# Handing out one branch's gates earlier, in the mixing stage of a two-block model

## The chip, the cores and the metric

One core of a Trainium2 chip runs the whole program. The metric is the device time of one execution in microseconds (us). TensorE (PE) multiplies matrices, VectorE (DVE), ScalarE (ACT) and GpSimd (POOL) work elementwise, and SyncE (SP) issues all DMA transfers from one queue, in order. PE has two clock levels, 2.4 and 1.2 GHz; the profile shows them as a granted clock of 1.0 and 0.5.

## The reference

A model of two blocks works on x of 512 tokens x 1024 channels in float32. The first block has two layers of attention, cross attention and a gated feed-forward part. The second block, where the change is, mixes the tokens in three branches of width 512, gates each and sums them:

```
h = rms_norm_2(x, norm_mix[l])
p_rw, p_s5, p_gla, p_gate = _split_2(h @ w_in[l], IN_SIZES)
y_rw = rwkv7_mix(p_rw, ...)     # a recurrence over tokens, 8 heads
y_s5 = s5_mix(p_s5, ...)        # a state space, 32 groups, and a gated projection
y_gla = gla_mix(p_gla, ...)     # gated linear attention in chunks of 64
gates = sigmoid(p_gate).reshape(B, L, 3, 1024)
merged = (gates[:, :, 0] * (y_rw @ w_branch[l, 0])
          + gates[:, :, 1] * (y_s5 @ w_branch[l, 1])
          + gates[:, :, 2] * (y_gla @ w_branch[l, 2]))
x = x + merged @ w_out[l]
```

Cross attention, a convolved feed-forward part and a last norm follow.

## The kernel before

All activations lie transposed, as tiles of 128 channels x 512 tokens. A float32 product is made of three products of halves (`mm3`, L282 to L284): a weight tile is loaded by SP into a raw buffer (7 of them), cast to its high half on ScalarE (L312), and the low half is what VectorE subtracts (L314); five pairs of halves exist at a time. A projection's output tile over 1024 channels takes two such loads and 24 matmuls.

**The mixing stage** (`Second.mix`) has a main line and jobs. The main line is the recurrence (`rwkv`): its part a for tiles 0 to 3; the inverse (`rwkv_invert`), 30 rows of small VectorE products and sums (L1507, L1508), each of which needs the one before, then copies (L1515) and transfers through DRAM; then part b (`rwkv_b`), one pass for each of the tiles 2, 3, 0, 1, of 35 steps. The first sixteen steps of a pass are mostly independent of each other. Its second half is a chain: products (L1632, L1661, the "G products"), eight additions (L1666), six steps of two small matmuls (L1676) and one addition (L1677), then L1684, L1690, a sum (L460), a power on GpSimd (L468), a copy (L498), transposes (L510) and the result. Between its steps the main line calls `kit.fill`, which hands out work of the jobs.

**The planner** is a count of costs, made when the program is written, that decides the order in which instructions are issued. A job yields its cost after each piece: 512 x 1.3e-3 for three matmuls of a tile and one input tile, two of these at a time in a projection; a negative number means "not before so much more on the clock". Jobs have a kind. Kind 0 are plain projections, in the order in which they were pushed; kind 1 are the state space (`s5_g`), and, pushed when its recurrence is done, linear attention (`gla_g`); kind 2 are moves of data, and the inverse. `fill(us, own)` sets the clock on by `own`, then hands out pieces worth `us`, kinds 0 and 1 in turn as far as they are ready; if nobody is ready, the rest of the call goes unserved:

```
self.clock += own
until = self.clock + us - self.over
while self.clock < until:
    job = self.ready(2) or self.ready(1 - self.turn) or self.ready(self.turn)
```

Part a calls `fill(4.0)` after each step, the inverse `while inverse[0]: kit.fill(2.0)` (a row asks to wait 1.7), part b `kit.fill(1.0 + 0.6 * w, w)` with the step's cost w. The compiler behind it moves an instruction ahead where it expects its inputs earlier, but each engine then works in one fixed order.

`gates_g(b)` is a job of kind 0 that projects the gates of branch b: 8 tiles, each scaled by L2200 on VectorE and put through a sigmoid (L2201). `merge_g(b)` multiplies a branch's projection by its gates and adds it: as jobs for branches 1 (state space) and 2 (linear attention), 8 tiles over 4 input tiles; for branch 0 (the recurrence) it is the first thing after part b, and its products with the first three tiles need not wait for the last one. The order of kind 0 is: the recurrence's low-rank inputs and tiles, gates of branch 1, then (when the state space is done) merge 1 and gates of branch 2, then (when linear attention is done) merge 2 and gates of branch 0.

`kit.room("abcc", a=22, b=11, c=...)` gives the stage's work tiles: stream a is the main line's, b belongs to the jobs of kind 0, c to those of kinds 1 and 2. The gates stay in b until they are merged; so do the two tiles of the low-rank input of the recurrence's own gate, which part b reads (`self.gd`).

Of the kernel before, what the change touches and what calls it, by code (L numbers as in the profile page):

```python
# [1320 lines left out]
class Second:  # L1321
# [912 lines left out]
    def mix(self):  # L2234
        kit, I = self.kit, self.I
        self.xs = kit.xs
        self.merged, self.gates, self.O = {}, {}, []
        gla, s5 = [], []

        def branch1():  # L2240
            yield from self.s5_g(s5, lambda: kit.push(branch2(), kind=1))
            kit.push(self.merge_g(1, s5, g1))
            self.g2 = kit.push(self.gates_g(2))

        def branch2():
            yield from self.gla_g(gla)
            kit.push(self.merge_g(2, gla, self.g2))
            self.g0 = kit.push(self.gates_g(0))

        kit.push(branch1(), kind=1)  # L2250
        lora = kit.push(self.rwkv_lora())
        g1 = kit.push(self.gates_g(1))
        kit.fill(20.0)
        kit.need(lora)
        rw = self.rwkv()
        kit.flush()
        kit.run(self.merge_g(0, rw, self.g0))
        job = kit.push(self.memory(), kind=2, stream=1)
        emit = lambda c: lambda i, p: self.add(2 * c + i, p, "norm_xattn")
        kit.proj_late([(I["w_out"][c], self.O[:-1], emit(c)) for c in range(4)], lambda: self.O[-1])  # L2260
        kit.need(job)
# [171 lines left out]
def handover(kit, first, s):  # L2433


    nc = kit.nc
    gg = kit.t([128, 8], "gg", 1)
    nc.vector.tensor_tensor(gg, first.g_final, s.v["norm_mix"], op=ALU.mult)
    state = {}

    def take(m):
        x = first.x[m]
        kit.normed(m, x, gg[:, m : m + 1])
        sq = kit.f()
        nc.scalar.activation(sq, x, AF.Square, scale=first.g_final[:, m : m + 1])
        if m == 0:
            state["acc"] = sq
        else:
            nc.gpsimd.tensor_tensor(state["acc"], state["acc"], sq, op=ALU.add)

    def done():
        r1 = kit.t([128, 4], "r1", 1)
        nc.vector.tensor_copy(r1, kit.rstd())
        p = kit.sums(state["acc"], kit.ones, [tok(b) for b in range(4)])
        s.r = kit.t([128, 4], "rstd", 1)
        nc.vector.tensor_copy(s.r, kit.renorm(r1, p, D))
        s.rb = kit.spread_end(kit.spread_begin(s.r, 4), kit.keep("acc"))
        rb1 = kit.spread(r1, 4)
        s.x_dram = s.scratch([DT, 128, S])
        for m in range(DT):  # L2460
            x = kit.f()
            nc.vector.scalar_tensor_tensor(x, first.x[m], first.g_final[:, m : m + 1], rb1, op0=ALU.mult, op1=ALU.mult)
            nc.sync.dma_start(s.x_dram[m], x)

    return take, done
# [4 lines left out]
def program(tc, ctx, I, out):  # L2470
    kit = Kit(tc, ctx, I)
    f = First(kit)
    kit.banks(*APART)
    kit.room("abbb", a=26, b=31)
    V, P = kit.nc.vector, kit.nc.gpsimd
    f.begin()
    kit.by(P)
    f.mixer_ab()
    kit.by(V)
    kit.share(X_BOTH)  # L2480
    f.cross(0)
    kit.share(BOTH)
    kit.room("aaaa", a=50)
    f.ffn(0, f.g_mix[1])
    kit.share(APART[0])
    kit.by(V, P)
    kit.room("abbb", a=24, b=33)
    f.mixer_cd()
    kit.by(V)
    kit.share(X_BOTH)  # L2490
    f.cross(1)
    kit.banks(*LATE)
    kit.room("abbb", a=31, b=50-31)
    s = Second(kit)
    take, done = handover(kit, f, s)
    job = kit.push(s.s5_make_g())
    f.ffn(1, take)
    kit.need(job)
    done()
    kit.room("abcc", a=22, b=11, c=54-22-11)  # L2500
    s.reset = kit.load("reset")
    s.mix()
    kit.flow(SFLOW)
    s.cross()
    kit.room("aaaa", a=50)
    s.ffn()
    s.finish(out)
# [13 lines left out]
```

## Time and profile before

| | before |
|---|---|
| median of 3 runs | 2700.7 us (2699.12 to 2701.46) |
| the profiled execution | 2699.61 us, span 2697.8 us |
| PE busy | 2578.3 us, 96% of the span |
| DVE / ACT / POOL busy | 1596.4 us (59%) / 1179.2 us (44%) / 520.6 us (19%) |
| mean granted PE clock | 0.977 |

The span goes from the first to the last instruction of the profiled execution. Busy is the time in which an engine has an instruction of its own; matmuls overlap, so PE's busy time is not the time at its peak. Times in rows count from the span's start. In a row of the timeline the bracket says how long the engine had been idle before it, and what ended that.

### The profile page before, as it was taken

Reading aid. Unit: us, or ns where it says so; the run is one execution under the profiler, and the core shown is the slowest. Engines: PE = TensorE matmul, PEld = TensorE weight load, DVE = VectorE, ACT = ScalarE, POOL = GpSimd, SP = SyncE. Lnnn points to the kernel's source line nnn. Section 1 sums busy time; section 2 is a strip of 40 time slices with the busy share of each in tenths; the row PEclk is TensorE's granted clock in tenths of the full one; section 3 lists DMA queues with packets and bytes.
Section 4 is the critical chain, followed back from the end, with each engine's and each line's share of the span. In section 5 each row is a group of like instructions: output and inputs, shape, how many; then the busy total and the mean of one; then the engine's idle time right before and its main releaser. Section 6 shows DMA issues by size and latency. Waiting matters only on the chain. (4 is left out here: it accounts for less than half of the span.)

```text
span 2697.8 us, 37057 instructions
## 1 busy us (share of the span) xinstructions
PE 2578.3 (96%) x13432; PEld 2087.6 (77%) x13432; DVE 1596.4 (59%) x3076; ACT 1179.2 (44%) x2208; POOL 520.6 (19%) x439
## 2 busy tenths in 40 slices
PE   8999999999999999999999989799999999999998
PEld 6668878888776787787877767587777798888886
DVE  5686654344447876876434577654463756774673
ACT  4576543233445765332434322435323545543442
POOL 5325121011211131243103232112230400100001
PEclk9999999999998999999999999899999999999999
DMA  4112223333322131344333553432222433233332
GB/s 155 36 52 86 67 82 95 98 97 93 118 90 70 45 95 51 107 125 141 126 106 110 170 168 100 97 98 63 67 79 65 127 120 96 83 97 96 98 94 69
DMA packets 172520, 258.51 MB, mean 96 GB/s; under 512 B 42528, under 2 KB 60832, under 8 KB 172320
## 3 DMA queue, kind: packets, MB, share of 16 engines
q1 hardware_dynamic: 172336, 256.13, 31.1%
q8 instruction: 106, 1.74, 0.3%
q14 instruction: 78, 0.64, 0.1%
HBM read 234.04 MB, written 22.15 MB: 95 GB/s over the span
## 5 line engine op out<-in xcount | busy, mean ns | idle before, releaser
L312 ACT CAST wh<-wraw 128x512 fp32r<-128x512 f32 (+1 forms) x777 | 473.0, 613 | 893.9 <-PE ps_mm L283 585.5
L314 DVE TENSOR_TENSOR wl<-wraw,wh 128x512 fp32r<-128x512 f32 (+1 forms) x691 | 493.8, 719 | 366.7 <-ACT wh L312 359.6
L284 PE MATMUL ps_mm<-xs,wl 128*128 128x512 f32 x1544 | 614.9, 398 | 23.0 <-DVE wl L314 21.4
L282 PE MATMUL ps_mm<-xs,wh 128*128 128x512 f32 x1544 | 626.2, 406 | 9.1 <-ACT wh L312 7.9
L283 PE MATMUL ps_mm<-xs,wh 128*128 128x512 f32 x1544 | 615.1, 398 | 2.3 <-DVE xs L264 2.2
L284 PEld LDWEIGHTS ps_mm<-xs,wl 128*128 128x128 f32 x1544 | 295.3, 191 | 91.0 <-DVE wl L314 24.1
L282 PEld LDWEIGHTS ps_mm<-xs,wh 128*128 128x128 f32 x1544 | 295.6, 191 | 77.2 <-ACT wh L312 8.3
L283 PEld LDWEIGHTS ps_mm<-xs,wh 128*128 128x128 f32 x1544 | 295.2, 191 | 66.2 <-DVE xs L264 6.0
L448 POOL TENSOR_TENSOR acc<-acc,za 128x512 f32<-128x512 f32 x59 | 83.7, 1419 | 719.6 <-ACT za L444 717.9
L282 PE MATMUL ps_mm<-za,wh 128*128 128x512 f32 x428 | 170.4, 398 | 3.4 <-DVE zb L2216 3.4
L284 PE MATMUL ps_mm<-za,wl 128*128 128x512 f32 x428 | 168.8, 394 | 4.1 <-DVE wl L314 4.1
L314 POOL TENSOR_TENSOR wl<-wraw,wh 128x512 fp32r<-128x512 f32 x86 | 112.5, 1316 | 308.4 <-ACT wh L312 303.7
L283 PE MATMUL ps_mm<-za,wh 128*128 128x512 f32 x428 | 167.6, 392 | 0.0
L1193 POOL TENSOR_TENSOR za<-za,za 128x512 f32<-128x512 f32 x44 | 60.0, 1364 | 461.2 <-ACT za L1192 461.2
L282 PE MATMUL ps_mm<-zb,wh 128*128 128x512 f32 (+1 forms) x284 | 100.4, 354 | 4.4 <-ACT zb L248 4.4
L245 DVE TENSOR_TENSOR za<-ps_tr,za 128x512 fp32r<-128x512 f32 (+3 forms) x152 | 84.6, 558 | 32.9 <-ACT za L248 31.8
L284 PEld LDWEIGHTS ps_mm<-za,wl 128*128 128x128 f32 x428 | 81.1, 190 | 23.5 <-DVE wl L314 4.5
L283 PE MATMUL ps_mm<-zb,wh 128*128 128x512 f32 (+1 forms) x284 | 97.4, 344 | 0.1
L284 PE MATMUL ps_mm<-zb,wl 128*128 128x512 f32 (+1 forms) x284 | 97.4, 343 | 0.0
L282 PEld LDWEIGHTS ps_mm<-za,wh 128*128 128x128 f32 x428 | 81.2, 190 | 20.2 <-DVE zb L2216 3.8
L283 PEld LDWEIGHTS ps_mm<-za,wh 128*128 128x128 f32 x428 | 81.2, 190 | 17.9
L468 POOL TENSOR_TENSOR rs<-sm,neghalf 128x4 f32<-128x4 f32 (+2 forms) x32 | 45.3, 1417 | 241.0 <-DVE sm L467 239.9
(606 smaller groups left out, 4823.7 us busy)
## 6 DMA issues: line engine op xcount, KB each, us to landing
wraw<-w_gu SPq DMA_DIRECT2D x176, 256.0 KB, 2.7
wraw<-w_dn SPq DMA_DIRECT2D x96, 256.0 KB, 2.6
wraw<-w_up SPq DMA_DIRECT2D x88, 256.0 KB, 2.6
wraw<-w_gate SPq DMA_DIRECT2D x48, 256.0 KB, 2.7
wraw<-w_dn SPq DMA_DIRECT2D x48, 192.0 KB, 2.3
dram<-za SPq DMA_DIRECT2D x26, 256.0 KB, 2.5
zc<-dram SPq DMA_DIRECT2D x26, 256.0 KB, 4.5
wraw<-w_cd SPq DMA_DIRECT2D x24, 256.0 KB, 2.6
```

Source lines behind the costliest of these rows:

```text
L245: self.nc.vector.tensor_tensor(lo, src, hi.bitcast(F32), op=ALU.subtract)
L282: mm(out, ah, bh, start=start, stop=False, **kw)
L283: mm(out, ah, bl, start=False, stop=False, **kw)
L284: mm(out, al, bh, start=False, stop=stop, **kw)
L312: self.nc.scalar.copy(hl[0], raw)
L314: eng.tensor_tensor(hl[1], raw, hl[0].bitcast(F32), op=ALU.subtract)
L448: self.nc.gpsimd.tensor_tensor(self.acc[0], self.acc[0], sq, op=ALU.add)
L468: self.nc.gpsimd.tensor_tensor(r, ms, self.neghalf[:, :n], op=ALU.pow)
L1193: nc.gpsimd.tensor_tensor(a, a, st["rb"], op=ALU.mult)
```

## The change

The gates of branch 2 are pushed right behind those of branch 1, before the recurrence begins. The gates of branch 0 take the place behind merge 1. Since 16 gate tiles can now be held at once, stream b gets 18 tiles instead of 11; a and c keep 22 and 21.

```
         def branch1():
             yield from self.s5_g(s5, lambda: kit.push(branch2(), kind=1))
             kit.push(self.merge_g(1, s5, g1))
-            self.g2 = kit.push(self.gates_g(2))
+            self.g0 = kit.push(self.gates_g(0))
 
         def branch2():
             yield from self.gla_g(gla)
             kit.push(self.merge_g(2, gla, self.g2))
-            self.g0 = kit.push(self.gates_g(0))
 
         kit.push(branch1(), kind=1)
         lora = kit.push(self.rwkv_lora())
-        g1 = kit.push(self.gates_g(1))
+        g1, self.g2 = (kit.push(self.gates_g(b)) for b in (1, 2))
         kit.fill(20.0)
...
     done()
-    kit.room("abcc", a=22, b=11, c=54-22-11)
+    kit.room("abcc", a=22, b=18, c=21)
     s.reset = kit.load("reset")
     s.mix()
```

## Rows read from the trace of the kernel before

**Rows 1.** Windows: us; PE, PEld, DVE, ACT, POOL busy; clock; DMA share, GB/s.
```profile
1663.00:1723.00 60.00, 43.85 (x303) 32.79 (x302) 45.23 (x117) 14.05 (x22) 11.87 (x8) 0.89 0.49 122
1770.00:1842.00 72.00, 70.42 (x513) 58.16 (x512) 34.97 (x72) 35.33 (x58) 11.64 (x11) 1.00 0.27 82
2120.00:2130.00 10.00, 10.00 (x45) 8.20 (x45) 3.77 (x6) 2.78 (x6) 2.42 (x3) 1.00 0.36 101
```

**Rows 2.** Waits of PE, 1590 to 2108: us in total, times, longest.
```profile
PE ps_mm L284 <- DVE wl L314: 15.3, 2, 14.6
```

**Rows 3.** Timelines of PE and ACT around 1690: start, us, engine, line.
```profile
1705.30 0.80 PE L284 MATMUL ps_mm<-xs,wl 128*128 128x512 f32 x1 [14.55 <-DVE wl L314]
...
1685.19 0.60 ACT L312 CAST wh<-wraw 128x512 fp32r<-128x512 f32 x1
```

**Rows 4.** Groups of DVE, 1663 to 1723: count, busy us, mean ns, idle before.
```profile
L1508 DVE TENSOR_TENSOR zc<-zc,zc 128x14 f32<-128x14 f32 (+35 forms) x44 | 13.2, 300 | 1.3
L1507 DVE TENSOR_TENSOR zc<-zc 128x14 f32<-128x14 f32 (+21 forms) x29 | 9.9, 340 | 0.9
L1507 DVE TENSOR_TENSOR zc<-zc,zc 128x16 f32<-128x16 f32 (+14 forms) x15 | 5.1, 342 | 0.4
L314 DVE TENSOR_TENSOR wl<-wraw,wh 128x512 fp32r<-128x512 f32 (+1 forms) x6 | 3.5, 609 | 0.0
...
L2200 DVE TENSOR_TENSOR zb<-ps_mm,acc 128x512 f32<-128x512 f32 x3 | 2.1, 685 | 4.1 <-PE ps_mm L284 4.1
```

**Rows 5.** Loads of w_gate (three windows) and w_br (one): ns, first to last issue.
```profile
L310 SPq DMA_DIRECT2D wraw<-w_gate x16: 327/382/463, 1589.1 to 1628.6; - x16
...
L310 SPq DMA_DIRECT2D wraw<-w_gate x16: 327/328/376, 1753.7 to 1865.6; - x16
...
L310 SPq DMA_DIRECT2D wraw<-w_gate x16: 327/328/333, 1925.4 to 2023.0; - x16
...
L310 SPq DMA_DIRECT2D wraw<-w_br x8: 327/328/328, 2026.5 to 2057.0; - x8
```

**Rows 6.** Windows with the clock at 0.50, columns as in rows 1.
```profile
1694.98:1708.63 13.65, 3.33 (x7) 2.10 (x7) 12.62 (x36) 2.18 (x4) 0.00 (x0) 0.50 0.44 94
2077.27:2087.51 10.24, 8.41 (x21) 6.35 (x22) 3.05 (x5) 1.25 (x3) 1.62 (x2) 0.50 0.14 51
```

**Rows 7.** Windows of tile 3's end, tile 0's and tile 1's second half.
```profile
1913.00:1958.00 45.00, 39.92 (x321) 32.17 (x314) 21.83 (x39) 11.64 (x25) 13.84 (x11) 0.96 0.13 41
1966.00:2000.00 34.00, 30.52 (x251) 24.04 (x247) 24.05 (x45) 7.33 (x13) 16.39 (x14) 1.00 0.27 87
2048.00:2084.00 36.00, 32.61 (x276) 26.18 (x274) 15.57 (x40) 9.25 (x17) 2.93 (x2) 0.91 0.25 74
```

**Rows 8.** Timelines of DVE and PE at the chain's six steps.
```profile
2058.66 2.03 DVE L1666 TENSOR_TENSOR za<-ps_ch,za 64x128 f32<-64x128 f32 x8 [1.68 <-issue]
...
1913.80 0.43 PE L1676 MATMUL ps_ch<-za,za 128*128 128x64 f32 x2
1915.03 0.43 PE L1676 MATMUL ps_ch<-za,za 128*128 128x64 f32 x2 [0.27 <-DVE za L1677]
...
2070.55 0.33 PE L1676 MATMUL ps_ch<-za,za 128*128 128x64 f32 x2
```

**Rows 9.** Timeline of PE at the end of tile 1's pass.
```profile
2070.81 1.15 PE L1684 MATMUL ps_ch<-za,za 64*64 64x64 f32 x32
...
2072.22 0.39 PE L282 MATMUL ps_si<-zc,wh 128*128 128x512 f32 x1
...
2072.92 1.02 PE L1690 MATMUL ps_ch<-za,center 128*128 128x512 f32 x2
...
2074.63 1.05 PE L460 MATMUL ps_ch<-half,za 128*128 128x2 f32 x8
2078.22 1.09 PE L510 MATMUL ps_ch<-ident,za 128*128 128x128 f32 x4 [2.54 <-DVE za L498]
```

**Rows 10.** Timeline of PE: linear attention's products in tile 0's pass.
```profile
1936.75 2.05 PE L1818 MATMUL ps_si<-zc,zc 128*128 128x128 f32 x16
```

More of the change, by code (lines that the diff above doesn't have):

```diff
@@ L2242, in branch1 @@
             kit.push(self.merge_g(1, s5, g1))
-            self.g2 = kit.push(self.gates_g(2))
+            self.g0 = kit.push(self.gates_g(0))
         def branch2():
@@ L2247, in branch2 @@
             kit.push(self.merge_g(2, gla, self.g2))
-            self.g0 = kit.push(self.gates_g(0))
         kit.push(branch1(), kind=1)
         lora = kit.push(self.rwkv_lora())
-        g1 = kit.push(self.gates_g(1))
+        g1, self.g2 = (kit.push(self.gates_g(b)) for b in (1, 2))
         kit.fill(20.0)
@@ L2499, in program @@
     done()
-    kit.room("abcc", a=22, b=11, c=54-22-11)
+    kit.room("abcc", a=22, b=18, c=21)
     s.reset = kit.load("reset")
```

## The prediction, as it was put on record

> **What bounds the kernel now.** Read the page first: TensorE (PE) is busy 96% of the span of 2697.8 us, so a change of order can only win PE's idle time and its time at the lower clock, or add to them. The change touches the mixing stage alone, so the windows come next, cut by what PE computes. One stretch stands out: from 1663 to 1723 us PE is busy 43.85 of 60 us, while in a pass of the recurrence, at 1770 to 1842, it is busy 70.42 of 72 [rows 1]. The table of waits gives that idle time one address: PE waited for the low half of a weight (L314 on VectorE, DVE), 15.3 us in two waits, 14.6 of them in one [rows 2]. The timeline has the spot: PE stops at 1690.75 and goes on at 1705.30, and the cast that this half needed had ended on ScalarE at 1685.8, 19 us before [rows 3]. So neither the load nor ScalarE was late: DVE was. Its groups in this stretch are led by the row operations of the inverse (L1507, L1508), 13.2 + 9.9 + 5.1 = 28.2 us [rows 4], and it is busy 45.23 of the 60 us [rows 1]. The subtract stood behind the rows in DVE's order.
>
> Last, the order of the handed-out jobs, by the loads of w_gate: 16 from 1589 to 1629 us (the gates of branch 1, called first gates here), 16 from 1754 to 1866 (second gates, branch 2), 16 from 1925 to 2023 (last gates, branch 0) [rows 5].
>
> **The change, part by part.** It removes and adds no instruction: the same 48 loads, casts, subtracts, matmuls and sigmoids come in another order. What it changes is who covers whom, so I add up the planner's own costs by its own rules. A gate tile costs 8 x 512 x 1.3e-3 = 5.3, a branch's gates 42.6, a merge 21.3. Before, the inverse's loop begins at clock 156, and the first gates end at 181; until the state space ends at 252 there is only kind 1, which mostly waits, and the loop's calls ask for 24 us that nobody has. The loop hands out 60. The four passes (tiles 2, 3, 0, 1) then get 53, 44, 36 and 43; 10 goes unserved in the last seven steps of tile 3, 19 in the first fifteen of tile 0, 11 in the last eight of tile 1. After the change the loop hands out 70, 33 of it second gates, and no call of it goes unserved. The passes get 54, 55, 27 and 31: the end of tile 3 and the start of tile 0 are served, but 26 goes unserved in steps 15 to 32 of tile 0, and 23 in the last sixteen of tile 1. So the holes don't vanish, they move: out of the inverse and out of a stretch of independent steps, into the serial halves of two passes.
>
> *Gain in the inverse.* The hole is 14.55 us [rows 3]. To fill it there are the 9.5 us more that are handed out, and up to five weights that can be split ahead of the rows. But second gates bring DVE work: 33 / 5.3 = 6.2 tiles, each with two subtracts of 0.61 and a scaling of 0.69 [rows 4], 12 us; the 24 us of other work that leaves the loop takes one subtract along for each 2.7 us, 5 in all. So DVE's 45 becomes 52, and PE's 44 becomes 53 [rows 1]. Two engines that both need some 53 us, one in front of the other, leave some idle time. Bounds: 5 (the rows stay a block) and the whole 14.55. I take 10: a third of the 16 us that are idle here stays. With the hole goes its low clock: 13.65 us at 0.50, PE busy 3.33 of them, 1.7 lost [rows 6].
>
> *Gain from tile 3's end to tile 0's middle.* PE is idle 45 - 39.9 = 5.1 us in 1913 to 1958 [rows 7]; a served pass shows 1.6 in 72 [rows 1]. Gain 4 (2 to 5).
>
> *Loss in tile 0's second half.* One pass is a chain from the G products on: DVE's eight additions before the first step take 2.0 us; six steps take at best 1913.80 to 1915.03 = 1.23 each, with 0.33 of PE in it, so 5.4 idle [rows 8]; then come gaps of 1.0, 0.7 and 2.54 before L1690, L460 and L510 [rows 9]. That makes 11.6 us if nothing fills them; before, 34 - 30.5 = 3.5 of idle stood there [rows 7]. Linear attention's own products (16 of them in 2.05 us [rows 10]) now fall into these steps and can stand in the first wait. I take an idle of 8, a loss of 4.5 (0 to 8.1).
>
> *Loss at tile 1's end.* The same 11.6; before, 36 - 32.6 = 3.4 [rows 7]. The last merge stands next in line: its loads were issued from 2026.5 on [rows 5], and of its first products 36 matmuls go into banks that the pass doesn't use. At 45 in 10 us [rows 1] they are worth 8 us, part of which ran there before too, as the ps_si row shows [rows 9]. I take an idle of 7.5, a loss of 4 (0 to 8.2).
>
> *Clock.* Idle pieces go with low stretches: at 2077, 10.24 us at 0.50 with PE busy 8.41, 4.2 lost [rows 6]. I add 1 (0 to 6). The Trainium skill (TensorE: Matmul & The Clock Gate, "A second HAM failure mode: psum-queue depth-cycling") speaks against the change here: a TensorE that pauses often between groups of matmuls is switched to and fro between its two levels. The trace agrees in part: the unserved stretch from 1913 to 1958, with its pauses, has a mean clock of 0.96 [rows 7]; by the rule alone the sum would be that of the slower rival below.
>
> *18 tiles, and SP's queue.* Kind 0's stream must hold two tiles of the gate's low-rank input and 16 gates, 18 in all. The last gates take what the state space's merge has freed, and stand behind it in the queue, so no wait is added; if that fails, a gate tile waits for one merge step of 1.3 us, and only kind 0 stands behind it. On SP's queue 16 loads move ahead of the state space's and the inverse's transfers; an issue takes 0.38 us [rows 5], and one that must wait for a raw buffer holds up what is behind it by the 2.7 us in which PE uses up a weight. Hidden by the weights that are split already: cost nothing, at worst those few us inside the inverse.
>
> Sum: -10 - 1.7 - 4 + 4.5 + 4 + 1 = -6.2 us. The profiled execution, 2699.6 us with a span of 2697.8, becomes 2693.4; the median of the runs lies 1.1 above it, so 2694.5.
>
> **The rivals.**
> 1. *The hole stays.* DVE has the rows as one block ahead of the second gates' subtracts again, and more to do. For it: the cast 19 us early, its subtract still behind [rows 3]. Against it: the weights split ahead. Gain 5 instead of 11.7, the rest as above: -5 - 4 + 9.5 = +0.5, 2701.
> 2. *All of it is given back.* Both serial halves stay empty: 8.1 + 8.2 lost, clock 1, 15.7 gained: +1.6, 2702. For it: the gap of 2.54 before L510 stood although the last merge's products were in order [rows 9].
> 3. *Nothing is lost.* Next steps and the last merge fill the serial halves: -15.7, 2685. For it: the compiler's order already has the last merge's products among tile 1's last steps [rows 9].
> 4. *Slower: the serial halves run at 1.2 GHz.* Place: steps 15 to 34 of tiles 0 and 1. From the first of the six steps on a pass has 6 x 0.33 + 1.15 + 1.02 + 1.05 + 1.09 = 6.3 us of its own PE work [rows 8, 9], its products before that about as much (an estimate from the same rows): 12, which half the clock doubles, in both passes 24. Half of that granted at 1.2 GHz adds 12: +6, 2707; all of it 2719. It decides once more than 6 us of PE work are added, 12 us of busy PE at 0.50 in these halves. Against it: the clock of 0.96 above.
>
> **How the numbers follow.** Forecast 0.43 (its own range 2689 to 2700), rival 1 0.17, rival 2 0.13, rival 3 0.15, rival 4 0.12. A measurement here tells about 0.2%, 5.4 us, from no change. Faster: a little over half of the forecast (0.26) and rival 3, 0.41. Within: the rest of the forecast (0.17) and most of rivals 1 and 2 (0.24), 0.41. Slower: rival 4 and what is left, 0.18. The range goes from rival 3 to the near end of rival 4, 2685 to 2707; beyond it lie half of each and little else.
>
> **What would show it.** Right: no wait of PE for L314 over 5 us in the inverse; the second 16 loads of w_gate begin before 1665; PE's idle time after the G products of tiles 0 and 1 up from 3.5 and 3.4 to about 8 each; PE's idle time in the stage down by 4 to 5 us. Wrong: a wait of 10 us or more for L314 (rival 1); steps at 1.23 us with nothing between them in both tiles (rival 2); steps of tile 1 among those of tile 0 (rival 3); a clock under 0.8 in the serial halves (rival 4). A hole elsewhere, as where the inverse's end waits for tiles of the third stream, would be none of these.

## The result, and the profile after

The changed kernel takes 2721.65 us (median of 4 runs, 2719.97 to 2725.54), the kernel before, run beside it, 2699.91 (4 runs): a ratio of 1.0083, 95% interval 1.0067 to 1.0099. It is slower by 22 us, outside the range of the prediction. The profiled execution took 2725.54 us with a span of 2723.8; it was 4.4 us behind the one before already at 358 us, far ahead of the mixing stage, and is 4.6 us late when the inverse begins, so its times are compared from there on. Line numbers behind L2243 are one lower than before.

**The inverse.** PE's waits from 1590 to 2133 and, in a second view, the timelines of PE and ACT around the hole, to be set beside [rows 2, 3]:

```profile
PE ps_mm L284 <- DVE wl L314: 16.6, 3, 15.6
...
PE ps_ch L1393 <- POOL zc L1778: 7.2, 2, 5.1
```

```profile
1690.15 0.50 PE L282 MATMUL ps_mm<-xs,wh 128*128 128x512 f32 x1 [2.33 <-ACT wh L312]
...
1706.47 0.79 PE L284 MATMUL ps_mm<-xs,wl 128*128 128x512 f32 x1 [15.58 <-DVE wl L314]
...
1688.96 0.63 ACT L2201 ACTIVATE zb<-zb 128x512 f32<-128x512 f32 x1 [11.34 <-DVE zb L2200]
1689.50 1.64 ACT L312 CAST wh<-wraw 128x512 fp32r<-128x512 f32 x3
1711.27 0.63 ACT L2201 ACTIVATE zb<-zb 128x512 f32<-128x512 f32 x1 [20.13 <-DVE zb L2200]
```

The hole is still there, one us longer than before, with the same releaser. And the last row shows a second engine in it: ScalarE stood 20 us at a sigmoid whose scaling VectorE had not done, and no weight behind it was cast.

The loads of w_gate, beside [rows 5]: one load of the second gates comes right behind the first ones, the other 31 from 1675.1 on, in one row where there were two.

```profile
L310 SPq DMA_DIRECT2D wraw<-w_gate x17: 327/382/393, 1593.4 to 1633.4; - x17
...
L310 SPq DMA_DIRECT2D wraw<-w_gate x31: 327/328/440, 1675.1 to 1881.1; - x31
```

**The passes.** Windows with the columns of [rows 1]: the inverse and a pass, to be set beside [rows 1], then tile 3's end and the second halves of tiles 0 and 1, beside [rows 7], each moved by as much as its first step is later; last two windows at 0.50, beside [rows 6].

```profile
1667.62:1727.62 60.00, 42.09 (x278) 31.57 (x273) 42.91 (x114) 8.88 (x17) 7.75 (x5) 0.86 0.37 100
1785.12:1857.12 72.00, 69.95 (x527) 58.09 (x525) 32.62 (x64) 21.45 (x42) 8.23 (x9) 1.00 0.26 80
1932.33:1977.33 45.00, 38.17 (x222) 29.42 (x221) 29.81 (x40) 21.68 (x32) 13.88 (x9) 0.94 0.20 58
1998.36:2032.36 34.00, 30.54 (x317) 24.92 (x317) 15.62 (x39) 8.14 (x16) 10.63 (x11) 0.92 0.19 63
2069.29:2105.29 36.00, 26.64 (x230) 19.88 (x228) 17.30 (x40) 8.71 (x18) 9.66 (x11) 0.72 0.07 19
1692.40:1709.47 17.07, 3.00 (x7) 2.42 (x8) 15.56 (x50) 0.00 (x0) 0.00 (x0) 0.50 0.06 16
2084.93:2112.24 27.31, 18.80 (x77) 13.74 (x78) 9.23 (x17) 5.80 (x12) 6.17 (x6) 0.50 0.00 1
```

Tile 1's end is the worst of it: PE idle 9.4 of 36 us, before 3.4, at a mean clock of 0.72, before 0.91. The timeline of PE there, beside [rows 8, 9]:

```profile
2081.25 0.50 PE L284 MATMUL ps_si<-zc,wl 128*128 128x512 f32 x1 [1.03 <-DVE wl L314]
...
2084.00 0.41 PE L1676 MATMUL ps_ch<-za,za 128*128 128x64 f32 x2 [1.78 <-DVE za L1673]
...
2085.79 0.66 PE L1676 MATMUL ps_ch<-za,za 128*128 128x64 f32 x2 [0.41 <-DVE za L1677]
2086.85 0.66 PE L1676 MATMUL ps_ch<-za,za 128*128 128x64 f32 x2 [0.41 <-DVE za L1677]
...
2092.22 2.08 PE L1690 MATMUL ps_ch<-za,center 128*128 128x512 f32 x2 [0.79 <-DVE za L1686]
...
2099.39 1.09 PE L510 MATMUL ps_ch<-ident,za 128*128 128x128 f32 x4 [2.54 <-DVE za L498]
...
2107.35 1.22 PE L282 MATMUL ps_mm<-zc,wh 128*128 128x512 f32 x2 [3.04 <-ACT zc L248]
...
2133.35 0.80 PE L282 MATMUL ps_mm<-za,wh 128*128 128x512 f32 x1 [4.91 <-DVE zb L2216]
```

The steps follow each other with nothing between them, and each product takes twice its time (L1690 2.08 us, before 1.02). The 27.31 us at 0.50 begin at the second of these steps, behind pauses of 1.03 us (for a weight) and 1.78 us (for L1673), and last through eight more, of 0.3 to 3.0 us. The Trainium skill (TensorE: Matmul & The Clock Gate, "A second HAM failure mode: psum-queue depth-cycling") says that a TensorE that idles often between groups of matmuls is switched between its levels; here the trace agrees in part: the level falls among such pauses, but it stays low instead of going to and fro. By half of PE's busy time there, an estimate, the lower level cost 18.8 / 2 = 9.4 us.

**Where the 22 us are.** I cut both traces at the same events (first and last row of the inverse, first L1676 of each pass, end of the last merge, eighth addition of w_out) and take PE's idle time, and half of its busy time in intervals granted 0.50 (an estimate), as lost:

| stretch | before: idle, low clock | after | more |
|---|---|---|---|
| the inverse's rows | 13.7, 0.0 | 17.9, 1.4 | +5.6 |
| to tile 2's first step | 6.7, 3.4 | 6.0, 3.2 | -0.9 |
| to tile 3's | 2.1, 1.7 | 3.7, 0.0 | -0.1 |
| to tile 0's | 5.6, 1.6 | 7.1, 2.9 | +2.8 |
| to tile 1's | 5.8, 1.7 | 6.9, 4.8 | +4.2 |
| to the last merge's end | 6.8, 4.8 | 13.5, 10.0 | +11.9 |
| to w_out's end | 0.0, 1.1 | 0.0, 2.5 | +1.4 |
| sum | 54.9 | 79.8 | +24.9 |

The stretch as a whole grows from 491.2 to 513.2 us, 22.0, which is the whole difference. The sum overshoots it by 3 us, so its rows are good for sizes and no more; half of it lies behind tile 1's first step. By kind, idle time grew from 40.7 to 55.1 us and the loss to the low clock from 14.2 to 24.7. The first two rows belong together: in the kernel before, the end of the hole and its low clock lie behind the last row operation and count in the second row. Over the 60 us windows above, which hold the hole whole, PE's idle time grew by 1.8 us only (16.2 to 17.9).

### The profile page after: what moved, and what is told of

It reads as the page before. It is cut to its first block, busy times and chain, and to the rows that moved or that the text cites. A ratio compares the mean times of both kernels' runs of the same rounds, so it can differ in the third digit from the quotient of the medians.

```text
span 2723.8 us, 37055 instructions
## 1 busy us (share of the span) xinstructions
PE 2590.8 (95%) x13432; PEld 2095.9 (77%) x13432; DVE 1600.3 (59%) x3076; ACT 1176.4 (43%) x2205; POOL 522.2 (19%) x439
## 4 chain that ended last, share of the span: by engine, by line
PE 51%; DVE 5%; issue 5%; POOL 2%; ACT 1%; DMA 0%; SPq 0%; POOLq 0%; DVEq 0%; ACTq 0%
PE ps_mm L282 14%; PE ps_mm L284 14%; PE ps_mm L283 14%; DVE wl L314 1%; POOL rs L468 1%; PE ps_ch L637 1%; PE ps_ch L282 0%; DVE zc L1507 0%; PE ps_ch L510 0%; PE ps_ch L283 0%; PE ps_ch L284 0%; PE ps_si L282 0%; DVE zc L1508 0%; PE ps_si L284 0%; PE ps_si L283 0%
## 5 line engine op out<-in xcount | busy, mean ns | idle before, releaser
L314 DVE TENSOR_TENSOR wl<-wraw,wh 128x512 fp32r<-128x512 f32 (+1 forms) x691 | 493.7, 718 | 396.0 <-ACT wh L312 381.3
L282 PE MATMUL ps_mm<-xs,wh 128*128 128x512 f32 x1544 | 624.7, 405 | 11.8 <-ACT wh L312 10.4
L282 PEld LDWEIGHTS ps_mm<-xs,wh 128*128 128x128 f32 x1544 | 295.5, 191 | 81.0 <-ACT wh L312 11.3
L314 POOL TENSOR_TENSOR wl<-wraw,wh 128x512 fp32r<-128x512 f32 x86 | 112.5, 1316 | 306.8 <-ACT wh L312 302.0
```

Source lines behind the costliest of these rows:

```text
L282: mm(out, ah, bh, start=start, stop=False, **kw)
L314: eng.tensor_tensor(hl[1], raw, hl[0].bitcast(F32), op=ALU.subtract)
```

## The experiments

The theories, by the letters that the expectations use. **T**: calls that nobody serves cost time in a serial half, tile 1's above all, since the last gates are used up before it. **D**: the hole stays because VectorE has the rows as one block ahead of the work that is handed out (**D2**: in two links, the subtract and the gates' scaling). Rivals: **R**, the room of 18 tiles costs the time; **G**, the second gates in the inverse do; **M** and **N**, the early work of the memory's job (`memory`, which loads, scales and splits the second input of the cross attention that follows) costs something, or nothing; **E**, another engine holds the hole; **C**, the chain's own length sets the end. Each run stands beside runs of the kernel before on the same chip; where two experiments are compared, it is by their ratios, times 2700 us. Where the intervals of two such ratios overlap, the difference alone proves little; this is said where it happens.

| run | median us | ratio to before, interval |
|---|---|---|
| e1, room alone | 2705.92 | 1.0029 (1.0016 to 1.0042) |
| e2, second gates alone | 2696.16 | 0.9994 (0.9981 to 1.0007) |
| e3, last gates alone | 2715.06 | 1.0052 (1.0034 to 1.0070) |
| e4, after, subtract on GpSimd | 2718.25 | 1.0069 (1.0055 to 1.0083) |
| e5, after, memory held back | 2713.05 | 1.0058 (1.0036 to 1.0079) |
| e6, after, order 2, 3, 0, 1 | 2709.46 | 1.0041 (1.0028 to 1.0054) |
| e7, after, VectorE free | 2715.52 | 1.0064 (1.0042 to 1.0085) |
| e8, e2 with VectorE free | 2693.62 | 0.9977 (0.9961 to 0.9994) |
| e9, before, order 2, 3, 0, 1 | 2695.00 | 0.9983 (0.9972 to 0.9995) |
| e10, after, e5 + e6 + e7 | 2700.21 | 1.0004 (0.9996 to 1.0013) |
| e11, e2 with all three | 2692.72 | 0.9971 (0.9960 to 0.9982) |
| e12, before, VectorE free and order | 2701.02 | 1.0011 (1.0001 to 1.0021) |

**e1: the room alone.** On the kernel before:

```
-    kit.room("abcc", a=22, b=11, c=54-22-11)
+    kit.room("abcc", a=22, b=18, c=21)
```

> The kernel before with 18 tiles instead of 11 for the second stream (21 for the third), and every job in its old place. Theory T (the tail: the calls of tile 1's second half that nobody serves cost the time): within 3 us of before, 2698 to 2703, since TensorE's order is that of before; at most the memory's scalings, which now stand among tile 1's last steps on VectorE, add 1 to 3 us. Rival R (the room: work of the memory that starts earlier pushes the chain back, or the layout is worse): 10 us or more of the 22 lost, 2710 or above.

Measured: +7.8 us by the ratio, between the two theories. The order of PE's instructions is that of before, so the cause must lie in the other engines' work or in the layout. The profiled execution took 2701.84 us, 2.2 over that of before, so its trace shows only part of the 7.8. The window from tile 1's first step to the end of the last merge, of the kernel before, then of this one:

```profile
2062.71:2109.28 46.57, 39.78 (x188) 31.25 (x187) 23.90 (x37) 14.03 (x24) 13.37 (x9) 0.88 0.33 95
```

```profile
2060.95:2110.75 49.80, 38.19 (x188) 29.94 (x187) 29.30 (x45) 19.44 (x38) 18.84 (x16) 0.91 0.31 88
```

PE is idle 11.6 us in it, before 6.8. VectorE, ScalarE and GpSimd have more to do (24 becomes 29, 14 becomes 19, 13 becomes 19 us): the memory's job, whose tiles come from the same stream and which now finds seven free. Its four loads, of the kernel before, of e1 and of the changed kernel, with the first and the last issue:

```profile
L188 SPq DMA_DIRECT2D zb<-mem2T x4: 327/353/1483, 2067.7 to 2097.1; - x4
...
L188 SPq DMA_DIRECT2D zb<-mem2T x4: 382/383/1300, 2065.9 to 2069.9; - x4
...
L188 SPq DMA_DIRECT2D zb<-mem2T x4: 327/328/384, 2050.5 to 2058.2; - x4
```

Before, they got their tiles one after another, as the last merge freed them; with 18 tiles all four are out at once. In the changed kernel the job stands in the chain itself, as ACT's timeline at tile 1's end shows:

```profile
2103.56 0.42 ACT L2280 ACTIVATE zb<-zb 128x256 f32<-128x256 f32 x1 [0.41 <-POOL zb L2281]
2105.84 0.42 ACT L2280 ACTIVATE zb<-zb 128x256 f32<-128x256 f32 x1 [1.86 <-POOL zb L2281]
2106.28 0.51 ACT L263 ACTIVATE zb<-zb,vecs 128x256 fp32r<-128x256 f32 x1
2106.70 0.60 ACT L248 CAST zc<-za 128x512 fp32r<-128x512 f32 x1
```

The last row is tile 1's split, for which the last merge waits. Its input, L1704, was ready at 2105.82; two instructions of the memory stood in front of it, the first of them held by GpSimd.

**e5: the memory held back.** On the changed kernel, with its 18 tiles:

```
-        mems = [kit.load("", src=src) for src in I["mem2T"]]
+        mems = [kit.f() for _ in range(4)]
+        for z, src in zip(mems, I["mem2T"]):
+            nc.vector.tensor_copy(z[:, 0:1], self.O[0][0][:, 0:1].bitcast(F32))
+            nc.sync.dma_start(z, src)
```

> The changed kernel, with the loads of the memory's job held back until the first tile of the last merge is there (a copy of one column of it into each load's tile). Theory M (the seven free tiles let the memory's work start among tile 1's last steps, where its instructions stand in the chain's way on VectorE, ScalarE and GpSimd): 2.3 us back between the pass's last scaling and its split and 1.7 us back in the last merge, 2716 to 2719. Rival R (the room costs as much as the median of the 18-tile run says): 2711 to 2715. Rival N (the memory costs nothing): 2720 to 2723.

Measured: 1.0058 against 1.0083, -6.7 us, about what the room alone had cost in e1. The two intervals overlap, so it is the trace that decides: the stretch from tile 1's first step to the end of the merge falls from 50.5 to 45.4 us.

```profile
2075.81:2121.20 45.39, 34.91 (x154) 26.68 (x155) 20.67 (x32) 10.18 (x18) 13.12 (x9) 0.77 0.20 56
```

With the layout of 18 tiles unchanged, that is most of the room's price: the room costs because it lets the memory in. The median lies in R's range, and the time by the ratio (2715.7) between R's and M's: theory M has the cause, but its price of 4 us, read off the chain alone, was rather too small.

**e2 and e3: one move each**, both with 18 tiles. e2 leaves the last gates behind linear attention's merge; e3 leaves the second ones behind the state space's:

```
# e2
-            self.g2 = kit.push(self.gates_g(2))
...
-        g1 = kit.push(self.gates_g(1))
+        g1, self.g2 = (kit.push(self.gates_g(b)) for b in (1, 2))
# e3
-            self.g2 = kit.push(self.gates_g(2))
+            self.g2, self.g0 = (kit.push(self.gates_g(b)) for b in (2, 0))
...
-            self.g0 = kit.push(self.gates_g(0))
```

> One move alone: the second gates right behind the first, the last gates still behind linear attention's merge, 18 tiles. By the planner's sums the inverse's calls are all served, 26 of planner time goes unserved in the first 18 steps of tile 3 and 27 in steps 5 to 23 of tile 0, nothing in tile 1. Theory T: the hole in the inverse stays (PE idle 16 to 20 us from 1663 to 1723, VectorE's low half the releaser), the unserved steps are independent ones and cost about 5 us in each of the two tiles, tile 1's end gains 2 to 4: 2698 to 2708. Rival G (the second gates in the inverse are what costs): 2712 or above. If the hole were filled, 2690 to 2695.

> The other move alone: the second gates behind the state space's merge as before, and the last gates right behind them, 18 tiles. Inverse as before; 40 of planner time goes unserved in tile 1, steps 9 to 34, and nothing before it. Theory T: the loss is all in tile 1, PE idle 15 us or more after its G products with a long stretch at 0.50 clock, less a gain of 5 to 8 us in tiles 3 and 0: 2708 to 2720. Rival G (the second gates in the inverse are what costs): 2690 to 2700.

Measured: e2 no change (-1.6 us by the ratio; its median of 2696.2 lies between T's range and that of a filled hole), e3 +14, in T's range. Rival G is out. Theory T stands on the tail, and the 14 us of e3 hold the price of the room as well, since e3 too has 18 tiles. e2's hole is that of the changed kernel (first row, PE's wait in the inverse). The windows from tile 1's first step to the merge's end, of e2 and of e3, show the difference:

```profile
PE ps_mm L284 <- DVE wl L314: 15.6, 1, 15.6
...
2058.53:2115.31 56.78, 51.73 (x260) 41.84 (x259) 34.98 (x54) 24.79 (x47) 19.09 (x16) 0.97 0.35 105
```

```profile
2076.71:2126.90 50.19, 36.32 (x151) 27.80 (x152) 25.03 (x36) 14.18 (x28) 18.12 (x15) 0.74 0.17 46
```

With the last gates beside it, tile 1's end runs at 0.97 with 5 us idle; without them at 0.74 with 13.9 idle. e2's 53 of unserved planner time, most of it among independent steps, cost little idle time: 0.9 us more than before up to tile 3's first step, 0.1 up to tile 0's. But it was not free in every execution. The profiled one took 2705.9 us, 10 over the median, and the clock was at 0.50 for 23.89 us in the unserved steps at the start of tile 3's pass. The window from tile 2's first step to tile 3's, of e2 and of e8 (below), which has the same order there:

```profile
1830.15:1903.67 73.52, 70.52 (x558) 60.22 (x557) 34.05 (x70) 20.18 (x40) 16.98 (x15) 0.84 0.18 56
...
1825.64:1891.92 66.28, 61.84 (x558) 52.13 (x557) 33.68 (x70) 20.18 (x40) 16.97 (x15) 1.00 0.20 62
```

**e6 and e9: work for the tail.** The last merge summed over tiles 0, 1, 2 and then 3, though tile 1 is the last pass: of its first three tiles, the second is the one that comes last. Here it goes 2, 3, 0, then 1, on the changed kernel (e6) and on the one before (e9):

```
+            ys = [ys[t] for t in (2, 3, 0, 1)]
...
-    o["w_br0"] = chunked(w_branch_2[0][0], 256)
+    o["w_br0"] = chunked(np.concatenate([w_branch_2[0][0][256:], w_branch_2[0][0][:256]]), 256)
```

> The changed kernel, with the last merge's sums taken over the tiles in the order 2, 3, 0 and then 1, instead of 0, 1, 2 and then 3, the rows of its weights laid out to match. Tile 1 is the last pass, so 36 products instead of 12 can go ahead of its end. Theory T (the tail loses because TensorE has nothing beside the chain): 24 products of 0.22 us, 5 us, move into TensorE's idle 13.5 us and raise its clock: 2713 to 2718. Rival C (the chain's own length sets the end, and products ahead of it only delay it): 2720 or above.

> The kernel before with the last merge's sums over the tiles in the order 2, 3, 0, 1. In its tail (from tile 1's first of the six steps to the end of the last merge) TensorE is idle 6.8 us and loses 4.8 to the low clock, in the changed kernel 13.5 and 10.0, of which this order took 13.8 away. Theory T (the order pays in the measure in which the tail is empty): about half of that, 4 to 7 us, 2691 to 2695. Rival (the order pays the same wherever it stands, so it says nothing on this change): 10 us or more, below 2689.

Measured: e6 -11.3 us (1.0041 against 1.0083), more than expected; e9 -4.6 by its ratio, as expected. The same window, of the changed kernel and of e6, then of e9:

```profile
2084.00:2134.50 50.50, 36.98 (x152) 28.16 (x153) 25.24 (x37) 14.19 (x28) 18.09 (x15) 0.71 0.18 46
...
2078.32:2115.76 37.44, 30.02 (x152) 22.65 (x153) 22.87 (x36) 13.66 (x28) 19.01 (x15) 0.92 0.23 60
```

```profile
2069.51:2109.84 40.33, 35.32 (x188) 28.21 (x187) 23.76 (x37) 13.83 (x24) 13.81 (x9) 0.98 0.40 109
```

In e6 products that had stood behind the pass now stand among its steps (27 between the first step and L510, where the changed kernel has one): the stretch is 13.1 us shorter, with 6.1 us less of idle time (13.5 becomes 7.4) and 7.7 less lost to the low clock (10.0 becomes 2.3). I had sized the first alone. The clock pays as much as the work does. Rival C is out. Of the 11.3 us, 4.6 are what the order gives the kernel before too; 6.7 belong to the change.

**e4 and e7: the hole.** e4 has the low halves subtracted on GpSimd during the loop; e7 takes the gates' scaling off VectorE as well (the lines with `apart`, which begins as False):

```
+        kit.by(kit.nc.gpsimd)
+        self.apart = True
         while inverse[0]:
             kit.fill(2.0)
+        self.apart = False
+        kit.by(kit.nc.vector)
...
-            nc.vector.tensor_tensor(s, p, self.rb, op=ALU.mult)
+            if self.apart:
+                nc.scalar.copy(s, p)
+                nc.gpsimd.tensor_tensor(s, s, self.rb, op=ALU.mult)
+            else:
+                nc.vector.tensor_tensor(s, p, self.rb, op=ALU.mult)
```

> The changed kernel with the low halves of the weights that are handed out during the inverse's loop subtracted on GpSimd instead of VectorE. Theory D (the hole stays because VectorE has the rows as one block ahead of the subtracts): the hole of 15.6 us falls to under 5, PE idle in the inverse from 20 to under 8 us, its low clock goes with it, and the time falls by 10 to 14 us, to 2708 to 2712. Rival E (another engine or the buffers of the raw weights are late as well): the hole keeps 10 us or more under another releaser, 2718 to 2724.

> The changed kernel, with all of the handed-out work off VectorE during the inverse's loop: the low halves are subtracted on GpSimd, and a gate tile is copied by ScalarE and scaled by GpSimd. Theory D2 (two links held the hole: the subtract, and behind it the gates' scaling, for which ScalarE's sigmoid waited in front of the next casts): no wait of PE over 4 us in the inverse, PE idle there under 6 us, 2708 to 2714. Rival E (a third thing is late, or the rows' length sets it): the hole keeps 7 us or more, 2716 to 2722.

Measured: e4 -3.8 us, e7 -5.1, both with intervals that overlap the changed kernel's, so the traces have to carry the argument. In e4 the hole halves and changes its releaser. PE's waits in the inverse, and ACT's timeline:

```profile
PE ps_mm L282 <- ACT wh L312: 9.7, 2, 7.4
...
1707.04 0.63 ACT L2203 ACTIVATE zb<-zb 128x512 f32<-128x512 f32 x1 [21.46 <-DVE zb L2202]
1707.58 0.80 ACT L312 CAST wh<-wraw 128x128 fp32r<-128x128 f32 x2
```

The gates' scaling (L2202 here, L2200 before) stands behind the rows just as the subtract did, the sigmoid waits for it, and the casts wait behind the sigmoid: neither D nor E alone, but both links. In e7, with both gone, PE's longest wait in the inverse is 2.4 us and its idle time among the rows 3.3 us, as D2 said. The time is not what D2 said (by the ratio 2717.3, in E's range), because the rows became slower. The window of the rows, the groups of VectorE (to be set beside [rows 4], whose times for L1507 and L1508 the changed kernel repeats), and timelines of the two engines:

```profile
1656.71:1715.67 58.96, 55.63 (x364) 41.54 (x362) 46.90 (x98) 13.92 (x25) 30.02 (x22) 1.00 0.50 131
...
L1508 DVE TENSOR_TENSOR zc<-zc,zc 128x14 f32<-128x14 f32 (+35 forms) x44 | 21.3, 485 | 1.3
L1507 DVE TENSOR_TENSOR zc<-zc 128x14 f32<-128x14 f32 (+21 forms) x29 | 12.8, 440 | 6.0 <-DMA zc<-dram 5.0
L1507 DVE TENSOR_TENSOR zc<-zc,zc 128x16 f32<-128x16 f32 (+14 forms) x15 | 6.6, 443 | 0.4
...
1671.88 1.23 DVE L1508 TENSOR_TENSOR zc<-zc,zc 128x64 f32<-128x64 f32 x1
...
1670.87 2.16 POOL L2206 TENSOR_TENSOR zb<-zb,acc 128x512 f32<-128x512 f32 x1 [0.16 <-DVE zc L1507]
```

The rows take 40.7 us instead of 28.2, and the loop 59 instead of 41.5, of which 5 are a wait for its load. The 15 us that PE won there it gives back in part: what follows the rows comes later, and until tile 2's first step PE now loses 9.9 idle and 9.5 to the low clock, in the changed kernel 6.0 and 3.2. Counted from one and the same matmul ahead of the inverse (at 1597.85 us in the changed kernel, 1591.97 in e7), tile 2's first step comes 5.3 us earlier.

**e8, e10, e11, e12: put together.** e8 is e2 with e7's edit; e10 the changed kernel with the edits of e5, e6 and e7; e11 is e2 with the three; e12 the kernel before with the edits of e6 and e7.

> The kernel with the second gates alone moved (the last gates behind linear attention's merge), 18 tiles, and the handed-out work off VectorE during the inverse's loop as in the kernel above. Theory D2 with theory T: the hole's 15 us are filled and the tail is served, so 8 to 13 us less than the 2696 of that move alone: 2683 to 2689, faster than both kernels. If what the inverse wins is given back in the unserved steps of tiles 3 and 0: 2692 to 2697.

> The changed kernel with three edits at once: the handed-out work off VectorE in the inverse's loop (6 us alone), the last merge's order 2, 3, 0, 1 (12 us alone) and the memory's loads held back (9 us alone). If the three places are apart and are all of the loss, the prices add: 2721.7 - 27 = 2695, 2692 to 2698. If order and held-back loads fill the same idle time of the tail: 2699 to 2705. If more of the loss lies in tile 0's serial half (7 us by its idle time and clock) it stays in either case.

> The second gates alone moved, 18 tiles, with the same three edits. Its tail is served by the last gates, so the order has little to fill (idle 5.0, clock 0.6): from 2693.6 without order and held-back loads 2 to 6 us less, 2687 to 2692. If the order pays wherever it stands: 2683 or below.

> The kernel before, none of the change's moves, with the handed-out work off VectorE in the inverse's loop and the last merge's order 2, 3, 0, 1. If the hole of 14.6 us is filled without the second gates, and paid in part by slower rows beside GpSimd as in the changed kernel: 2 to 6 us from the inverse and what the order alone gives: 2687 to 2693. If there is not enough work in the loop without the second gates, the inverse gives nothing: what the order alone gives, 2692 to 2696.

Measured: e10 is back at the time of before, 1.0004: the three give 1.0083 - 1.0004 = 21 us together, against 6.7 + 11.3 + 5.1 = 23 one by one. So they hardly overlap, though the median lies in the range for an overlap: the 2695 that I expected without one came of medians measured beside different runs of the kernel before. That is time won back, not a bill of the change: the order wins 4.6 in the kernel before too, and a hole of 14.6 us stood there as well. As an estimate, the change's own price is 6.7 (order) + 6.7 (memory) + 4.7 (the first two rows of the table), 18 of the 22 us. With the 7 us that stay open below it is more than the whole: these are sizes, not a sum that closes. e11 is faster than the kernel before by 0.29% (0.18 to 0.40), e8 by 0.23% (0.06 to 0.39). e8 lies where it was said to lie if the unserved steps take back what the inverse wins, e11 just above its range. In e11's tail, which the last gates serve, order and held-back loads give 1.6 us only, no clear difference, against 18 in the changed kernel's. e12 missed both of its ranges: it is at 1.0011 of the kernel before (1.0001 to 1.0021), and 7.6 us slower than e9, the order alone. It shows why the hole is no matter of one instruction. PE's longest wait in its inverse, and ACT's timeline there:

```profile
PE ps_si L282 <- ACT zc L248: 17.2, 1, 17.2
...
1707.72 0.62 ACT L248 CAST zc<-zc 16x512 fp32r<-16x512 f32 x1 [17.20 <-DVE zc L1751]
```

With subtracts and gates off VectorE, linear attention's first scaling (L1751) is what stands behind the rows now: a hole of 17 us again.

## Why the prediction was wrong

*Gain in the inverse, -10 and -1.7 of clock.* This step failed first. It took the hole for a lack of handed-out work and filled it with more of it. But the hole is VectorE's order, and each tile of the new work brings two more subtracts and a scaling to the same queue. Rival 1 had the mechanism; it got 0.17, and its sign, a wait of 10 us or more for L314, is there with 15.6. Measured: +4.7 up to tile 2's first step (+1.8 idle in the 60 us window, with 1.5 lost to the low clock against 1.7) instead of -11.7. e4 and e7 show the links one by one; in e7, where they are gone, PE's idle time there is 3.3 us.

*Gain from tile 3's end to tile 0's middle, -4.* Not there: the window's idle time is 6.8 us, before 5.1. The second half of linear attention now falls here and leaves a wait of its own, 5.1 us for L1778 on GpSimd. Served by the planner's sums is not served by the engines.

*Loss in tile 0's second half, +4.5.* The idle time stayed at 3.5, but the clock fell from 1.00 to 0.92, which costs some 2.5 of the 30.5 busy us. Up to tile 1's first step the loss is 4.2 us, most of it the clock: the size was right, the kind was not.

*Loss at tile 1's end, +4.* The mechanism was right and the size was off: idle +6.0 in the window (9.4, forecast 7.5), but with the low clock +11.9 up to the merge's end. The near hit in the window is in part luck: the six steps leave 1.5 us idle in all, not 5.4, because they come 0.8 to 1.06 us apart and not 1.23; and the sum left out the waits behind the pass, 3.04 us for tile 1's split (before 0.88) and 4.91 at the merge's end (before 3.37). Two more numbers were wrong. The 36 matmuls of the last merge that were to go ahead are 12, because the merge's order has the last pass second; e6 puts the 24 back and wins 11.3 us. And rival 4's price was taken as another case with a chance of 0.12, where it is what this empty tail brought with it: 10.0 us in place of 4.8, at a clock of 0.72 in the window, under the 0.8 of rival 4's sign.

*Clock, +1, and -1.7 in the inverse.* The worst term after the inverse: over the whole stretch the low clock took 10.4 us more (14.2 becomes 24.7), half of that at tile 1's end; most of it is part of the sizes given above.

*18 tiles, 0.* Wrong: 7.8 us (e1), 6.7 (e5, less certain). I asked who would wait for a tile of this stream and not who would get one early. The memory's job did.

*The range.* Its upper end of 2707 was rival 4 with all other terms as forecast. The rivals were priced one at a time; hole, tail and room went wrong together.

What stays open: the 7 us from tile 3's first step to tile 1's were seen in the trace (the wait for L1778, the clock) and not tried by a run of their own; e10's trace holds 5.3 of them still, and makes them good in the tail (8.3 us lost, before 11.6) and, by 1 us, up to tile 2's first step.

## What to carry to other kernels

A hole that ends at an engine's queue is not filled by more work that passes through the same queue: look for what stands in front of the late instruction, and for every engine that would wait behind it. Unserved steps cost little idle time where steps are independent (though in one execution of e2 the clock fell there too), and most in a serial tail; keep independent work for the tail, and sum in the order in which the parts come ready. When a pool grows, ask which later job will start early in it, and what it will stand in front of.

## What the hardware showed

In e7, 25 of the 88 row operations of VectorE overlap in time with an instruction of GpSimd. These took 12.5 us longer, in sum, than the same rows of the changed kernel (up to 1.1 us for one); the other 63 differ by 0.03 us in sum. In e4 it is 10 rows and 4.0 us. The 128x64 row above ended at 1673.11, just behind GpSimd's L2206 (the scaling of a gate tile) at 1673.03. The Trainium skill (SBUF — State Buffer, "SBUF: two separate sides") says that a VectorE operation with two SBUF inputs and a GpSimd operation that reads SBUF exclude each other for a whole instruction; the trace agrees, and in this kernel it makes GpSimd a poor place for work beside the chain of small rows.

TensorE's clock took three quarters of what its idle time did in the tail: 10.0 us (an estimate, as above) against 13.5. After a stretch of short pauses it stayed at 0.50 for 27.31 us, of which PE was busy 18.80; and with products put among the same steps (e6) the tail's loss fell to 2.3 us. The low level also lasted where PE did not pause: in the 25 us from 1851 in e2, at a mean clock of 0.52, PE was busy 24.99.
